# Top-2 dispatch on one core: row groups of 67 and 61 without an early store, in place of 65 and 63 with one

## The chip, the cores and the metric

The kernel runs on one core of one Trainium2 chip. The metric is the device time of one execution in microseconds. All transfers between the chip's main memory (HBM) and the on-chip memory (SBUF, 128 partitions) go through the core's 16 DMA engines; VectorE (DVE) and ScalarE (ACT) compute; SyncE (SP) and ACT issue transfers.

## What is computed

For each of 16 x 1024 tokens there are 8 router logits and a row of 512 float32 values. The two largest softmax probabilities are normalised to a sum of 1, and the row is written twice, scaled by each of the two weights, the smaller one first.

```python
probs = np.exp(router_logits - logits_max)
probs = probs / np.sum(probs, axis=-1, keepdims=True)
topk_indices = np.argsort(probs, axis=-1)[..., -k:]          # k = 2
topk_probs = np.take_along_axis(probs, topk_indices, axis=-1)
topk_probs = topk_probs / np.sum(topk_probs, axis=-1, keepdims=True)
x_expanded = x[:, :, np.newaxis, :].repeat(k, axis=2)
return (x_expanded * topk_probs[..., np.newaxis]).astype(np.float32)
```

So 33.6 MB of rows are read and 67.1 MB are written: each row that comes in goes out twice.

## The kernel before, in words

**Tiling.** 16384 tokens are 128 rows for each of the 128 partitions. They are handled in two groups, `GROUPS` (L16): 65 rows per partition, then 63. Within a group each partition owns consecutive tokens, so what one DMA moves for a partition is one contiguous piece. "A row" below means one row in each of the 128 partitions: 262,144 bytes of input and twice that of output.

**Homes.** `xs` (L97) holds one group's rows, one slot of 2 KB a row and partition; group 1 reuses the slots of group 0. `osp` (L98) has `OSP` output rows of 4 KB. Before the first output needs them, its last row holds the logits and the two rows before that the scratch space of the weights (L101, L102). A store's product lies either in `osp`, or in `xs` itself ("x"): the output pairs are written over input slots already used, and two slots hold one output row.

**Order.** For each group the loop at L109 first lists the loads of `LOADS[g]` (L112), one DMA each on SP's queue. In group 0 the logits come right behind the first load (L105, L106), and `top2_weights` (L53 to L68) finds the two largest logits by a small tournament on DVE; two sigmoids on ACT of their difference give the weights `WA`. Then come the stores of `STORES[g]`. Each has a count of rows, a home, `by_act` and a queue: one DVE multiplication (L127) does all rows but the last `by_act`, which ACT does in two copies a row (L135). Then the DMA at L138 goes out on the queue named.

In the texts, loads are numbered 1 to 5 and the stores on SP's queue by their order. Before, group 0 has loads 1 to 3 (6, 28, 31 rows), an early store of 2 rows, the only DMA issued by ACT, and stores 1 to 4 (16, 16, 16, 15 rows); group 1 has loads 4 and 5 (32, 31 rows) and stores 5 to 8 (16, 16, 16, 15).

**What orders the work.** The framework puts in the waits from the slots that instructions share. A multiplication waits for the load of its rows. Stores alternate between `osp` and `xs`, so the multiplication for an `osp` store waits until the previous `osp` store has landed. A load of group 1 waits until the stores from the slots it overwrites have landed. SP takes its instructions in order: what waits at its head holds up all behind it.

Of the kernel before, what the change touches and what calls it, by code (L numbers as in the profile page):

```python
# [1 line left out]

# [4 lines left out]

F32 = mybir.dt.float32
ALU = mybir.AluOpType
ACTF = mybir.ActivationFunctionType  # L10
P = 128
E = 8
D = 512


GROUPS = [65, 63]  # L16
M = sum(GROUPS)


LOADS = [[6, 28, 31], [32, 31]]  # L20


STORES = [
    [
        (2, ("osp", 0), 0, "ACT"),
        (16, ("osp", 2), 0, "SP"),
        (16, ("x", 2), 0, "SP"),
        (16, ("osp", 0), 4, "SP"),
        (15, ("x", 35), 0, "SP"),
    ],  # L30
    [
        (16, ("osp", 0), 1, "SP"),
        (16, ("x", 0), 0, "SP"),
        (16, ("osp", 0), 4, "SP"),
        (15, ("x", 33), 0, "SP"),
    ],
]
OSP = 18


def top2_weights(nc, scratch, logits, WA):

    used = [0]

    def cut(n):
        a = scratch[:, used[0] : used[0] + M * n].rearrange("p (m n) -> p m n", n=n)
        used[0] += M * n
        return a

    a, b = logits[:, :, 0:4], logits[:, :, 4:8]  # L50
    hi = cut(4)
    lo = b
    nc.vector.tensor_tensor(hi, a, b, op=ALU.max)  # L53
    nc.vector.tensor_tensor(lo, a, b, op=ALU.min)  # L54
    n = 4
    while n > 1:
        n //= 2
        a, b = hi[:, :, 0:n], hi[:, :, n : 2 * n]
        nhi, nlo, tmp = cut(n), cut(n), cut(n)
        nc.vector.tensor_tensor(tmp, lo[:, :, 0:n], lo[:, :, n : 2 * n], op=ALU.max)  # L60
        nc.vector.tensor_tensor(nlo, a, b, op=ALU.min)  # L61
        nc.vector.tensor_tensor(nlo, nlo, tmp, op=ALU.max)  # L62
        nc.vector.tensor_tensor(nhi, a, b, op=ALU.max)  # L63
        hi, lo = nhi, nlo
    dlt = cut(1)
    nc.vector.tensor_tensor(dlt, hi, lo, op=ALU.subtract)  # L66
    nc.scalar.activation(WA[:, :, 0], dlt[:, :, 0], ACTF.Sigmoid, scale=-1.0)  # L67
    nc.scalar.activation(WA[:, :, 1], dlt[:, :, 0], ACTF.Sigmoid, scale=1.0)  # L68


@with_exitstack
def kernel(
    ctx: ExitStack,
    tc: tile.TileContext,
    x: bass.AP,
    router_logits: bass.AP,
    k: bass.AP,
    out: bass.AP,
):
    nc = tc.nc  # L80
    N = x.shape[0] * x.shape[1]
    assert int(k) == 2 and router_logits.shape[-1] == E and x.shape[2] == D
    assert N == P * M
    xf = x.rearrange("b s d -> (b s) d")
    of = out.rearrange("b s k d -> (b s) k d")
    rf = router_logits.rearrange("b s e -> (b s) e")
    x_v, o_v, rl_v = [], [], []
    t0 = 0
    for n in GROUPS:
        t1 = t0 + P * n  # L90
        x_v.append(xf[t0:t1].rearrange("(p m) d -> p m d", p=P))
        o_v.append(of[t0:t1].rearrange("(p m) k d -> p m k d", p=P))
        rl_v.append(rf[t0:t1].rearrange("(p m) e -> p m e", p=P))
        t0 = t1

    pool = ctx.enter_context(tc.tile_pool(name="pool", bufs=1))
    xs = pool.tile([P, max(GROUPS), D], F32)  # L97
    osp = pool.tile([P, OSP, 2, D], F32)  # L98
    WA = pool.tile([P, M, 2], F32)

    logits = osp[:, OSP - 1].rearrange("p k d -> p (k d)").rearrange("p (m e) -> p m e", e=E)  # L101
    scratch = osp[:, OSP - 3 : OSP - 1].rearrange("p r k d -> p (r k d)")  # L102

    def load_logits():
        nc.sync.dma_start(logits[:, : GROUPS[0]], rl_v[0])  # L105
        nc.sync.dma_start(logits[:, GROUPS[0] :], rl_v[1])  # L106

    m0 = 0
    for g, G in enumerate(GROUPS):  # L109
        r = 0  # L110
        for n in LOADS[g]:
            nc.sync.dma_start(xs[:, r : r + n, :], x_v[g][:, r : r + n, :])  # L112
            if g == 0 and r < 6 <= r + n:
                load_logits()
                top2_weights(nc, scratch, logits, WA)
            r += n
        assert r == G
        r = 0
        for n, (home, a), by_act, queue in STORES[g]:
            if home == "x":  # L120
                og = xs[:, a : a + 2 * n, :].rearrange("p (r k) d -> p r k d", k=2)
            else:
                og = osp[:, a : a + n]
            v = n - by_act
            w = WA[:, m0 + r : m0 + r + n, :]
            if v:
                nc.vector.tensor_tensor(  # L127
                    og[:, :v],
                    xs[:, r : r + v, :].unsqueeze(2).to_broadcast([P, v, 2, D]),
                    w[:, :v].unsqueeze(3).to_broadcast([P, v, 2, D]),  # L130
                    op=ALU.mult,
                )
            for i in range(v, n):
                for c in range(2):
                    nc.scalar.activation(  # L135
                        og[:, i, c], xs[:, r + i, :], ACTF.Copy, scale=w[:, i, c : c + 1]
                    )
            {"SP": nc.sync, "ACT": nc.scalar}[queue].dma_start(o_v[g][:, r : r + n], og)  # L138
            r += n
        assert r == G  # L140
        m0 += G


# [1 line left out]
_INS = ['x', 'router_logits', 'k']  # L145
_OUTS = [((16, 1024, 2, 512), 'float32')]

_NUMBERS = {'k': 2}


# [26 lines left out]
```

## Time and profile before

| | us |
|---|---|
| median of 3 runs | 239.23 (239.12 to 239.34) |
| the profiled execution: its own time | 239.38 |
| its span, first to last instruction | 237.6 |
| DVE busy in it | 132.2 (56%) |
| ACT busy in it | 13.2 (6%) |

The mean rate of the DMA engines over the span is 426 GB/s, reads and writes together. "q1" is the queue on which SP issues, "q10" that of ACT. In the timeline a row gives start, duration, engine (a "q" behind it: the issue of a DMA), line, operation, output and input, and in brackets how long the engine was idle before and what ended that. In the grouped lines the numbers behind the bar are the busy time, the mean of one in ns, and the idle time before. In the DMA issues the last number is the time from issue to landing. In the windows view, the last two columns are the share of the 16 DMA engines' time and the rate, of the packets that start in the stretch; a packet is what one partition moves in one DMA.

### The profile page before, as it was taken

The numbers are of one execution on the slowest core, as the hardware profiler recorded it, in microseconds if no ns is written. First come the engines' busy times: TensorE is split into PE (matmuls) and PEld (weight loads), VectorE is DVE, ScalarE is ACT, GpSimd is POOL, SyncE is SP. The second block draws the span as 40 slices with busy tenths as digits, with TensorE's granted clock in tenths as the row PEclk, the third lists the DMA queues.
The fourth block names the chain that finished last, engine by engine and source line by source line (L and its number), as shares of the span: only waits on it lengthen the run. The fifth ranks groups of instructions, "written<-read, shape, count | busy, mean of one in ns | idle before, by whom it ended". The sixth has DMA issues, their size and how long they took to land.

```text
span 237.6 us, 124 instructions
## 1 busy us (share of the span) xinstructions
DVE 132.2 (56%) x20; ACT 13.2 (6%) x21; POOL 0.2 (0%) x4
## 2 busy tenths in 40 slices
DVE  0640599999289999000000009999956999920000
ACT  2000000000080000000000001000006100000000
POOL 0000000000000000000000000000000000000000
DMA  7979989898989989899998989898989989897995
GB/s 265 541 338 488 408 386 535 348 530 353 496 386 441 441 353 530 353 508 414 414 519 353 508 370 502 353 519 353 496 386 419 463 353 530 353 530 342 496 445 217
DMA packets 2304, 101.19 MB, mean 426 GB/s; under 512 B 256, under 2 KB 384, under 8 KB 512
## 3 DMA queue, kind: packets, MB, share of 16 engines
q1 hardware_dynamic: 2160, 100.14, 97.7%
q10 hardware_dynamic: 144, 1.05, 1.0%
HBM read 34.08 MB, written 67.11 MB: 426 GB/s over the span
## 4 chain that ended last, share of the span: by engine, by line
DMA 48%; DVE 39%; SPq 1%; issue 0%; DVEq 0%
DMA xs<-in_x_dram 30%; DVE osp L127 25%; DMA out_dram<-osp 19%; DVE xs L127 14%; SPq L105 0%; SPq L106 0%; SPq L112 0%; SPq L138 0%; DVEq L127 0%
## 5 line engine op out<-in xcount | busy, mean ns | idle before, releaser
L127 DVE TENSOR_TENSOR osp<-xs,WA 128x12288 f32<-128x12288 f32 (+3 forms) x5 | 61.6, 12318 | 68.7 <-DMA xs<-in_x_dram 58.4
L127 DVE TENSOR_TENSOR xs<-xs,WA 128x16384 f32<-128x16384 f32 (+1 forms) x4 | 66.8, 16692 | 0.3
L135 ACT ACTIVATE osp<-xs,WA 128x512 f32<-128x512 f32 x18 | 11.4, 709 | 161.3 <-DMA out_dram<-osp 90.0
L53 DVE TENSOR_TENSOR osp<-osp 128x512 f32<-128x512 f32 x1 | 0.7, 692 | 8.2 <-DMA osp<-in_router_logits_dram 8.2
L67 ACT ACT_TABLE_LOAD x1 | 1.3, 1283 | 0.7 <-PEq L158 0.7
L67 ACT ACTIVATE WA<-osp 128x128 f32<-128x128 f32 x1 | 0.3, 316 | 10.1 <-DVE osp L66 10.1
L54 DVE TENSOR_TENSOR osp<-osp 128x512 f32<-128x512 f32 x1 | 0.7, 693 | 0.0
L60 DVE TENSOR_TENSOR osp<-osp 128x256 f32<-128x256 f32 (+1 forms) x2 | 0.7, 352 | 0.0
L62 DVE TENSOR_TENSOR osp<-osp 128x256 f32<-128x256 f32 (+1 forms) x2 | 0.7, 352 | 0.0
L63 DVE TENSOR_TENSOR osp<-osp 128x256 f32<-128x256 f32 (+1 forms) x2 | 0.7, 352 | 0.0
L61 DVE TENSOR_TENSOR osp<-osp 128x256 f32<-128x256 f32 (+1 forms) x2 | 0.7, 351 | 0.0
L66 DVE TENSOR_TENSOR osp<-osp 128x128 f32<-128x128 f32 x1 | 0.3, 292 | 0.0
L68 ACT ACTIVATE WA<-osp 128x128 f32<-128x128 f32 x1 | 0.3, 298 | 0.0
L158 POOL MEMSET const-bfloat16-1.0<- 128x1 bf16 x1 | 0.1, 102 | 0.0
L158 POOL MEMSET const-uint8-127<- 128x1 uint8 x1 | 0.1, 102 | 0.0
L158 POOL MEMSET const-float32-0.0<- 128x1 f32 x1 | 0.1, 99 | 0.2 <-issue 0.2
L158 POOL MEMSET const-float32-1.0<- 128x1 f32 x1 | 0.1, 99 | 0.0
## 6 DMA issues: line engine op xcount, KB each, us to landing
xs<-in_x_dram SPq DMA_DIRECT2D x2, 7936.0 KB, 40.8
out_dram<-xs SPq DMA_DIRECT2D x2, 7680.0 KB, 27.5
xs<-in_x_dram SPq DMA_DIRECT2D x1, 7168.0 KB, 24.2
xs<-in_x_dram SPq DMA_DIRECT2D x1, 1536.0 KB, 6.0
out_dram<-osp ACTq DMA_DIRECT2D x1, 1024.0 KB, 24.5
osp<-in_router_logits_dram SPq DMA_DIRECT2D x1, 260.0 KB, 6.2
osp<-in_router_logits_dram SPq DMA_DIRECT2D x1, 252.0 KB, 6.4
out_dram<-osp SPq DMA_DIRECT2D x4, 23.9
```

Of the source, the lines that this page charges most:

```text
L53: nc.vector.tensor_tensor(hi, a, b, op=ALU.max)
L54: nc.vector.tensor_tensor(lo, a, b, op=ALU.min)
L60: nc.vector.tensor_tensor(tmp, lo[:, :, 0:n], lo[:, :, n : 2 * n], op=ALU.max)
L61: nc.vector.tensor_tensor(nlo, a, b, op=ALU.min)
L62: nc.vector.tensor_tensor(nlo, nlo, tmp, op=ALU.max)
L63: nc.vector.tensor_tensor(nhi, a, b, op=ALU.max)
L66: nc.vector.tensor_tensor(dlt, hi, lo, op=ALU.subtract)
L67: nc.scalar.activation(WA[:, :, 0], dlt[:, :, 0], ACTF.Sigmoid, scale=-1.0)
L68: nc.scalar.activation(WA[:, :, 1], dlt[:, :, 0], ACTF.Sigmoid, scale=1.0)
L127: nc.vector.tensor_tensor(og[:, :v], xs[:, r : r + v, :].unsqueeze(2).to_broadcast([P, v, 2, D]), w[:, :v].unsqueeze(3).to_broadcast([P, v ...
L135: nc.scalar.activation(og[:, i, c], xs[:, r + i, :], ACTF.Copy, scale=w[:, i, c : c + 1])
L158: nc = _bacc.Bacc("TRN2", target_bir_lowering=False, num_devices=1)
```

## The change

The groups become 67 and 61 rows. The early store on ACT's queue is taken out, all DMAs are issued by SP, and the rows are cut anew: group 0 has loads 1 to 3 of 6, 31 and 30 rows and stores 1 to 5 of 14, 13, 13, 13 and 14; group 1 has loads 4 and 5 of 31 and 30 rows and stores 6 to 9 of 15, 15, 16 and 15. `osp` has 16 rows in place of 18, `xs` 67 slots in place of 65. The tables name each load's slot and each store's first row and slot; as given, the slots are the same as the rows.

```diff
-GROUPS = [65, 63]
+GROUPS = [67, 61]
 M = sum(GROUPS)
-LOADS = [[6, 28, 31], [32, 31]]
+LOADS = [[(6, 0), (31, 6), (30, 37)], [(31, 0), (30, 31)]]
 STORES = [
     [
-        (2, ("osp", 0), 0, "ACT"),
-        (16, ("osp", 2), 0, "SP"),
-        (16, ("x", 2), 0, "SP"),
-        (16, ("osp", 0), 4, "SP"),
-        (15, ("x", 35), 0, "SP"),
+        (0, 14, 0, ("osp", 0), 0, "SP"),
+        (14, 13, 14, ("x", 0), 0, "SP"),
+        (27, 13, 27, ("osp", 0), 3, "SP"),
+        (40, 13, 40, ("x", 27), 0, "SP"),
+        (53, 14, 53, ("osp", 0), 4, "SP"),
     ],
     [
-        (16, ("osp", 0), 1, "SP"),
-        (16, ("x", 0), 0, "SP"),
-        (16, ("osp", 0), 4, "SP"),
-        (15, ("x", 33), 0, "SP"),
+        (0, 15, 0, ("osp", 0), 1, "SP"),
+        (15, 15, 15, ("x", 0), 0, "SP"),
+        (30, 16, 30, ("osp", 0), 4, "SP"),
+        (46, 15, 46, ("x", 31), 0, "SP"),
     ],
 ]
-OSP = 18
+OSP = 16
...
-        for n in LOADS[g]:
-            nc.sync.dma_start(xs[:, r : r + n, :], x_v[g][:, r : r + n, :])
+        for n, s in LOADS[g]:
+            nc.sync.dma_start(xs[:, s : s + n, :], x_v[g][:, r : r + n, :])
...
-        r = 0
-        for n, (home, a), by_act, queue in STORES[g]:
+        for r, n, s, (home, a), by_act, queue in STORES[g]:
...
-                    xs[:, r : r + v, :].unsqueeze(2).to_broadcast([P, v, 2, D]),
+                    xs[:, s : s + v, :].unsqueeze(2).to_broadcast([P, v, 2, D]),
...
-                        og[:, i, c], xs[:, r + i, :], ACTF.Copy, scale=w[:, i, c : c + 1]
+                        og[:, i, c], xs[:, s + i, :], ACTF.Copy, scale=w[:, i, c : c + 1]
```

More of the change, by code (lines that the diff above doesn't have):

```diff
@@ L135 @@
                     nc.scalar.activation(
-                        og[:, i, c], xs[:, r + i, :], ACTF.Copy, scale=w[:, i, c : c + 1]
+                        og[:, i, c], xs[:, s + i, :], ACTF.Copy, scale=w[:, i, c : c + 1]
                     )
             {"SP": nc.sync, "ACT": nc.scalar}[queue].dma_start(o_v[g][:, r : r + n], og)
-            r += n
-        assert r == G
         m0 += G
```

## The prediction

> **What bounds the kernel now.** I read the page first: the DMA queues, then the chain.
>
> ```profile
> span 237.6 us, 124 instructions
> ...
> DMA packets 2304, 101.19 MB, mean 426 GB/s; under 512 B 256, under 2 KB 384, under 8 KB 512
> ## 3 DMA queue, kind: packets, MB, share of 16 engines
> q1 hardware_dynamic: 2160, 100.14, 97.7%
> q10 hardware_dynamic: 144, 1.05, 1.0%
> ...
> DMA 48%; DVE 39%; SPq 1%; issue 0%; DVEq 0%
> ```
>
> The chain gives VectorE (DVE) 39%, which suggests that compute bounds a third of the time. The queues speak against it: the two together keep all 16 DMA engines busy for 98.7% of the span. The chain passes through DVE because it follows waits; where DVE is on it, the DMA engines are working off something queued earlier. To see whether a hole hides in the average, I asked the windows view for stretches cut at the places where packets begin. It counts a packet where it starts, so a short window can read 0.00 or far over 1 without meaning idle time or overload.
>
> ```profile
> core 0: us, DVE busy (x) ACT busy (x) POOL busy (x), PEclk, DMA share, GB/s
> 0.00:1.70 1.70, 0.00 (x0) 0.97 (x1) 0.20 (x4) 1.00 0.00 0
> 7.18:45.73 38.55, 25.46 (x14) 0.51 (x2) 0.00 (x0) 1.00 1.01 431
> 45.73:217.86 172.13, 106.72 (x7) 11.36 (x18) 0.00 (x0) 1.00 1.00 434
> ```
>
> From 45.73 on the share is 1.00 at 434 GB/s for 172 us: no hole in which a better order could win anything. At that rate 101.19 MB takes 233.2 us; with 1.7 us before the first packet that is 234.9 of the 237.6 us. All that any order of the same bytes can win lies in the remaining 2.7 us: the slow beginning, the 431 GB/s of the stretch from 7.18 to 45.73, and the end.
>
> **The change part by part.** The bytes stay: 128 rows in, 256 rows out, the logits. So do 5 loads of x, 2 of logits, 9 stores, and with them the packets (144 each). What could move is how evenly they follow each other.
>
> *The early store goes.* It is the only transfer of the second queue. Its issue (size, us to landing), then the first large multiplication, the issue of store 1 behind it, and that store's time to landing:
>
> ```profile
> out_dram<-osp ACTq DMA_DIRECT2D x1, 1024.0 KB, 24.5
> ```
>
> ```profile
> 26.35 17.23 DVE L127 TENSOR_TENSOR osp<-xs,WA 128x16384 f32<-128x16384 f32 x1 [11.43 <-DMA xs<-in_x_dram]
> 43.61 0.35 SPq L138 DMA_DIRECT2D out_dram<-osp  x1
> ```
>
> ```profile
> out_dram<-osp SPq DMA_DIRECT2D x1, 22.2
> ```
>
> Its 1 MB needs 24.5 us to land, mixed packet by packet with loads 2 and 3. One row of x is 262,144 bytes, 0.604 us at 434 GB/s; one output row is 1.208. Loads 2 and 3 (28 and 31 rows) and the early store (2 output rows, worth 4) are 63 rows, 38.05 us. The trace has 38.55 from the first packet of load 2 to the first of store 1: 0.50 us over. By the rates, 3 of 434 GB/s over 38.55 us is 0.27 us. This stretch is the only one with two queues and the only long one before the last store under 434. I read the excess as the price of switching between the queues and expect it to go: a gain of 0.27 to 0.50 us; I take **0.35**, nearer to the lower, since the first engine's packets exaggerate and the window also catches the last small packets of the logits. From below the bound is zero: if it belongs to the beginning, it stays. The DVE work and the ACT issue that it saves lay beside the loads and are worth nothing.
>
> A rule weighed against this: the Trainium skill, "DMA: Bandwidth & Descriptors", section "Issuing engines are not separate DMA queues", says that transfers issued by several engines run on the same 16 DMA engines and interleave, and that this saves only issue time; then dropping the second queue moves nothing, and the sum would be 0 in place of 0.35. The trace agrees on the interleaving (24.5 us to land); whether it is free is rival 1.
>
> *Store 1 starts when loads 2 and 3 are done: is it ready?* This was the early store's other service: it filled 2.4 us in which DVE worked. Durations of DVE:
>
> ```profile
> L127 DVE TENSOR_TENSOR xs<-xs,WA 128x16384 f32<-128x16384 f32 x2 | 34.5, 17225 | 0.1
> L127 DVE TENSOR_TENSOR xs<-xs,WA 128x15360 f32<-128x15360 f32 x2 | 32.3, 16158 | 0.2
> L127 DVE TENSOR_TENSOR osp<-xs,WA 128x12288 f32<-128x12288 f32 x2 | 25.9, 12958 | 9.8 <-DMA out_dram<-osp 9.8
> ```
>
> 16, 15 and 12 rows are 17.23, 16.16 and 12.96 us: 1.067 us a row and 0.15 once. So 14 rows take 15.1, 13 rows 14.0, 10 rows 10.8. Load 2 with 31 rows runs from 7.18 for 18.7 us: the first engine is through at 25.9. Engines are up to 0.5 us apart:
>
> ```profile
> 43.82:45.73 1.91, 1.91 (x1) 0.00 (x0) 0.00 (x0) 1.00 0.00 0
> 45.73:46.20 0.47, 0.47 (x1) 0.00 (x0) 0.00 (x0) 1.00 5.16 2231
> 157.97:159.90 1.93, 1.84 (x2) 0.00 (x0) 0.00 (x0) 1.00 0.00 0
> 159.90:160.35 0.45, 0.45 (x1) 0.00 (x0) 0.00 (x0) 1.00 5.40 2330
> ```
>
> so the last one ends near 26.4, and with an estimated 0.4 us to landing and 0.1 to DVE (store 1 before: 45.73 plus 16 rows is 65.06, the last engine 65.5, landed 43.61 plus 22.2, or 65.8), store 1's multiplication runs from 26.9 to 42.0. Load 3 (30 rows, 18.1 us) frees the first engine at 44.0. Slack from issue to need: 2.0 us. How much is enough? Before, store 1 was issued at 43.61 and began at 45.73, 2.1 us, without a hole; store 5 is the tighter case:
>
> ```profile
> 142.10 16.16 DVE L127 TENSOR_TENSOR osp<-xs,WA 128x15360 f32<-128x15360 f32 x1 [46.93 <-DMA xs<-in_x_dram]
> ...
> 158.32 0.34 SPq L138 DMA_DIRECT2D out_dram<-osp  x1
> ```
>
> issued at 158.32, first packet at 159.90: 1.6 us, share still 1.00. In an empty queue (first load, below) it is 1.0. So 2.0 suffices; the cover is 0.4 to 1.0 us.
>
> *Smaller stores on two homes.* Store 3 (13 rows into `osp`) and store 5 (14 rows) wait until the store two before has landed, as before:
>
> ```profile
> 65.95 12.96 DVE L127 TENSOR_TENSOR osp<-xs,WA 128x12288 f32<-128x12288 f32 x1 [5.11 <-DMA out_dram<-osp]
> 78.98 0.33 SPq L138 DMA_DIRECT2D out_dram<-osp  x1
> 79.01 16.16 DVE L127 TENSOR_TENSOR xs<-xs,WA 128x15360 f32<-128x15360 f32 x1
> ```
>
> Store 1 lasts 16.9 us to 60.9; landing by 61.8; DVE does 10 rows by 72.7 beside ACT's 3; store 2 (15.7 us) ends at 76.6: slack 3.9. Store 4 in place, 14.0 more: 86.7 against 92.3. Store 5: from 93.2, 10 rows by 104.1, against 108.0: 3.9. Nothing starves, so the sum here is 0. ACT's 24 copies in place of 18 stand beside DVE and are shorter:
>
> ```profile
> L135 ACT ACTIVATE osp<-xs,WA 128x512 f32<-128x512 f32 x18 | 11.4, 709 | 161.3 <-DMA out_dram<-osp 90.0 <-DMA xs<-in_x_dram 71.2
> ```
>
> 8 copies in at most 5.7 us beside 10.8.
>
> *Load 4 waits for a later store.* Its slots 0 to 30 now overlap stores 2 and 4 (slots 0 to 25, 27 to 52), formerly one store. Behind it on SP stand load 5 and the stores of group 1.
>
> ```profile
> 95.20 0.33 SPq L138 DMA_DIRECT2D out_dram<-xs  x1
> 95.58 27.65 SPq L112 DMA_DIRECT2D xs<-in_x_dram  x2
> ```
>
> ```profile
> SPq L112 <- DMA out_dram<-xs: 26.2, 1, 26.2
> ```
>
> Before, load 4 went out right after store 4 and load 5 sat 26.2 us on SP for that store. Now both wait, till about 108.9. Store 5, issued at 104.1 ahead of them, keeps the engines busy from 108.0 to 124.9: 16 us of cover; cost 0. If store 5 stood behind load 4, the cover would be gone: rival 3.
>
> *Group 1.* Load 4 (31 rows) ends at 143.6, load 5 (30 rows) at 161.7. Store 6 may start after load 4's landing: 144.5 plus 0.1 and 15.1 for DVE's 14 rows, 159.7: slack 2.0, against 1.6 before. Stores 7 to 9 have 4 us and more, by the same arithmetic. The last store has 15 rows as before, so the tail is unchanged.
>
> Sum: -0.35 against the profiled execution's 239.38, which gives 239.03. That execution lies 0.15 us over the median; from 239.23 it is **238.9 us**. The starting order, the 1.7 us before the first packet and the 1.8 us outside the span stay.
>
> **Rivals.**
>
> *1. No gain (239.2).* The excess of 0.27 to 0.50 us comes with the first long load, not with the second queue. For it: the beginning is slow anyway. Against: the only other long load-after-load stretch (loads 4 and 5) lies in the window at 434. Within 0.2%.
>
> *2. Store 1 comes late (240.0, slower).* Place: the end of load 3. The early store no longer stretches the loads, so if DVE issues store 1 later than 44.0 less the needed 1.0 to 1.6 us, that is after 42.4 to 43.0, all 16 engines stand still, and every microsecond is one of the kernel: nothing later has slack to give it back. Load 2 landing 1.5 us later than worked out would put the issue at 43.5 and cost up to 1.1: 240.0 with the 0.35 still won. Against it: before, 1.6 us of slack left no hole.
>
> *3. Load 4 is queued ahead of store 5 (240.9, slower).* The source lists store 5 first; whether the built program keeps that order on SP is not to be seen here. If not, load 4 waits at SP's head for store 4's landing at 108.9, its first packet comes 1.0 to 1.6 us later, and the engines stand from 108.0 to 109.9 or 110.5: 1.9 to 2.5 us.
>
> ```profile
> 0.73 0.38 SPq L112 DMA_DIRECT2D xs<-in_x_dram  x1
> ```
>
> (1.0 is this issue at 0.73 against the first packets at 1.70.) Against it: before, SP kept store 4 ahead of load 4, though load 4's own store had landed 10 us earlier (issue 60.87 plus 24.3, below).
>
> ```profile
> 60.87 0.34 SPq L138 DMA_DIRECT2D out_dram<-xs  x1
> ```
>
> ```profile
> out_dram<-xs SPq DMA_DIRECT2D x1, 7680.0 KB, 27.7
> out_dram<-osp SPq DMA_DIRECT2D x2, 23.9
> out_dram<-xs SPq DMA_DIRECT2D x1, 24.3
> ```
>
> **How the numbers follow.** 0.2% of 239.23 is 0.48 us, about what a measurement of this kernel can tell from no change; the limits are 238.75 and 239.71. Forecast 0.64: with the gain between 0.27 and 0.50, a spread of runs of 0.1 either way, and engines that end up to 0.5 us apart, 0.28 of it falls under 238.75 and 0.36 above. Rival 1, 0.20: same. Rival 2, 0.10, and rival 3, 0.06: slower. Faster 0.28, same 0.56, slower 0.16. The range 238.5 to 239.7 holds forecast and rival 1 with both bounds of the gain and leaves out rivals 2 and 3.
>
> **What would show it.** No q10; between the first packet of load 2 and that of store 1 about 36.8 us at 434 GB/s; store 1 issued near 42.0 and its first packets near 44.0 without a hole; store 5 ahead of load 4 on SP; share 1.00 to the last store. A window without packets longer than one packet (some 2 us) near 44, 109 or 162 would make the prediction wrong, as would a rate under 434 in a stretch that has no hole.

## The result, and the profile after

The changed kernel is a little slower. Its median is 239.78 us (239.46 to 240.26), that of the kernel before on the same chip 239.30 (239.12 to 239.34): a ratio of 1.0023 [1.0014, 1.0032]. Measured once more it had 239.54 (239.35 to 240.14) beside 239.37, 1.0011 [1.0002, 1.0019]. The loss is thus 0.2 to 0.5 us, and its runs spread over 0.8 us where those of the kernel before spread over 0.2. The profiled execution took 239.65 us, with a span of 237.9, 0.3 longer than before.

The page of the changed kernel:

```profile
span 237.9 us, 131 instructions
...
DMA packets 2304, 101.19 MB, mean 425 GB/s; under 512 B 256, under 2 KB 384, under 8 KB 512
q1 hardware_dynamic: 2304, 101.19, 98.7%
```

Bytes and packets are as before, on one queue now, and it is as full as the two were together (98.7%). The page doesn't tell where 0.3 us went. The windows view of the changed kernel does, cut where the first packet of a transfer starts (columns as in the prediction): loads 2 and 3; stores 1 to 4; store 5; load 4; load 5; stores 6 to 8.

```profile
7.34:44.17 36.83, 20.89 (x13) 0.52 (x2) 0.00 (x0) 1.00 1.01 436
44.17:108.19 64.02, 47.73 (x4) 8.80 (x14) 0.00 (x0) 1.00 1.00 434
108.19:125.49 17.30, 0.00 (x0) 0.00 (x0) 0.00 (x0) 1.00 1.00 424
125.49:144.20 18.71, 0.00 (x0) 0.00 (x0) 0.00 (x0) 1.00 1.00 434
144.20:162.32 18.12, 17.07 (x2) 1.34 (x2) 0.00 (x0) 1.00 1.00 434
162.32:217.86 55.54, 43.30 (x3) 5.12 (x8) 0.00 (x0) 1.00 1.00 434
```

Below, a transfer's *stretch* is the time from its own first packet to the first packet of the next one, on the earliest engine, and what a stretch takes beyond its bytes at 0.604 us a row is its *excess*. Loads 2 and 3 are 61 rows, 36.84 us: the stretch has 36.83, and the excess of before is gone. Store 5 is 14 output rows, 16.91 us, and takes 17.30: 0.39 over, at 424 GB/s and a share of 1.00. The engines don't stand; some of its packets take longer. In the kernel before, the last store of group 0 (15 rows, 18.12 us) has next to no such excess (0.04):

```profile
103.68:121.84 18.16, 0.00 (x0) 0.00 (x0) 0.00 (x0) 1.00 1.00 433
```

The windows view also tells which packets are slow. Where a window holds one packet's start on each of the 16 engines, its share times its length is the mean time of these packets. Of store 5 of the changed kernel, the last packets but one and the last ones:

```profile
120.87:121.31 0.44, 0.00 (x0) 0.00 (x0) 0.00 (x0) 1.00 4.81 2085
122.98:123.42 0.44, 0.00 (x0) 0.00 (x0) 0.00 (x0) 1.00 5.69 2085
```

The former take 4.81 x 0.44, or 2.12 us, the latter 5.69 x 0.44, or 2.50. The whole excess of 0.39 lies in the last packet of each engine.

Added up: the first packet of load 2 starts 0.16 later (7.34 against 7.18), the loads give 0.50 (38.55 less 38.05), store 5 takes back 0.35 (0.39 less 0.04). So the earliest engine begins the last store at 217.86 in both kernels. What is left of the 0.3 us lies with the other engines. Windows at the start of the last store, first of the kernel before, then of the changed one:

```profile
217.86:218.30 0.44, 0.00 (x0) 0.00 (x0) 0.00 (x0) 1.00 5.17 2234
```

```profile
217.86:218.30 0.44, 0.00 (x0) 0.00 (x0) 0.00 (x0) 1.00 3.88 1676
218.30:219.00 0.70, 0.00 (x0) 0.00 (x0) 0.00 (x0) 1.00 0.81 351
```

A packet is counted where it starts, and here each has 61,440 bytes. 2234 GB/s over 0.44 us is 16 packets, so before, all 16 engines begin the last store within 0.44 us. After, 12 do, and 4 come later (351 GB/s over 0.70 us). The latest engine sets the end.

The order on SP is the one that was foreseen. Timeline of the changed kernel, SP's issues (those before store 1, stores 2 to 4 and 7 to 9 left out):

```profile
42.19 0.35 SPq L139 DMA_DIRECT2D out_dram<-osp  x1
...
104.27 0.33 SPq L139 DMA_DIRECT2D out_dram<-osp  x1
109.10 1.64 SPq L114 DMA_DIRECT2D xs<-in_x_dram  x2
160.32 0.34 SPq L139 DMA_DIRECT2D out_dram<-osp  x1
```

### The profile page after: what moved, and what is told of

Same layout as the page of the kernel before. It is cut to its first block, busy times and chain, and to the rows that moved or that the text cites. A ratio compares the mean times of both kernels' runs of the same rounds, so it can differ in the third digit from the quotient of the medians.

```text
span 237.9 us, 131 instructions
## 1 busy us (share of the span) xinstructions
DVE 129.0 (54%) x20; ACT 17.1 (7%) x27; POOL 0.2 (0%) x4
## 3 DMA queue, kind: packets, MB, share of 16 engines
q1 hardware_dynamic: 2304, 101.19, 98.7%
## 4 chain that ended last, share of the span: by engine, by line
DMA 52%; DVE 35%; SPq 1%; issue 0%; DVEq 0%
DMA xs<-in_x_dram 26%; DVE osp L128 23%; DMA out_dram<-osp 17%; DVE xs L128 13%; DMA out_dram<-xs 9%; SPq L107 0%; SPq L108 0%; SPq L114 0%; DVEq L128 0%; SPq L139 0%
## 5 line engine op out<-in xcount | busy, mean ns | idle before, releaser
L128 DVE TENSOR_TENSOR osp<-xs,WA 128x14336 f32<-128x14336 f32 (+2 forms) x5 | 64.8, 12959 | 73.2 <-DMA xs<-in_x_dram 55.8
L128 DVE TENSOR_TENSOR xs<-xs,WA 128x13312 f32<-128x13312 f32 (+1 forms) x4 | 60.4, 15092 | 0.3
L136 ACT ACTIVATE osp<-xs,WA 128x512 f32<-128x512 f32 x24 | 15.3, 711 | 157.4 <-DMA out_dram<-osp 92.4
```

The lines of the kernel that those rows point to most:

```text
L128: nc.vector.tensor_tensor(og[:, :v], xs[:, s : s + v, :].unsqueeze(2).to_broadcast([P, v, 2, D]), w[:, :v].unsqueeze(3).to_broadcast([P, v ...
L136: nc.scalar.activation(og[:, i, c], xs[:, s + i, :], ACTF.Copy, scale=w[:, i, c : c + 1])
```

## The experiments

The question is what slows the last packets of store 5, and what the early store had to do with it. Ratios stand against the kernel before, timed on the same chip. Where letters stand in the expectations: A1 is the pile-up of two loads issued at once, A2 the pitch of the slots, B the time at which load 4 is queued, C the size of the last store, D a price that is paid once, at the first place where stores and loads meet, E one that each such place costs, F that a transfer queued before the last packets of the one ahead have started slows them.

### Is the gain that of the second queue, and is the loss that of the pile-up or the pitch?

**The changed kernel again.** No edit.

> The changed kernel as it is, for a second profile and more times. Theory A (a lasting cost where store 5's last packets meet the queued loads of group 1, 0.39 us a DMA engine in the first profile of it): the stretch from the first packets of store 5 to the last of load 4 is again about 0.4 us longer than its bytes at 434 GB/s, and the time lies 0.3 to 0.6 us over the kernel before (239.6 to 239.9). Rival (the excess was an accident of one execution, and the loss lies at the start or the end): that stretch is within 0.05 us of its bytes, and another one is long.

239.54 us, as told above. Store 5 has its excess again (17.29 against 16.91), and 15 of the 16 engines begin the last store in time:

```profile
108.17:125.46 17.29, 0.00 (x0) 0.00 (x0) 0.00 (x0) 1.00 0.99 425
217.86:218.30 0.44, 0.00 (x0) 0.00 (x0) 0.00 (x0) 1.00 4.85 2095
```

So the excess on the earliest engine came again, and the lag of the other engines differs between these two executions.

**The early store on SP's queue**, in the kernel before:

```diff
-        (2, ("osp", 0), 0, "ACT"),
+        (2, ("osp", 0), 0, "SP"),
```

> The kernel before with one edit: its early store of 2 rows goes out on SP's queue, behind load 3, in place of ACT's. Theory of the prediction (the second queue costs 0.35 to 0.37 us between the first packet of load 2 and the first of store 1): this gap is gone, and the time is 238.9 to 239.0. Rival (the excess belongs to the first long load or to the early store itself): 239.2 to 239.35, with the stretch still 0.3 to 0.5 us over its bytes.

240.19 us, 1.0036 [1.0023, 1.0049]: one queue, and slower. SP issues the early store at 15.19 us, behind load 3, so it no longer mixes with the loads. Loads 2 and 3 alone (59 rows, 35.64 us) take 36.61: an excess of 1.0 us with a single queue. The second row is the last store of group 0, 18.12 by its bytes:

```profile
7.20:43.81 36.61, 24.55 (x14) 0.51 (x2) 0.00 (x0) 1.00 1.01 426
104.22:122.33 18.11, 0.00 (x0) 0.00 (x0) 0.00 (x0) 1.00 1.00 434
```

The excess lies in load 3's last packets, behind which the early store stands. In the kernel before, it lies mostly in load 2's last packets, beside which the early store runs; load 3, which alternates with it, does not pay. The first row is load 3's last packets here; the other two are of the kernel before, load 2's last packets and then load 3 with the early store:

```profile
40.48:41.21 0.73, 0.73 (x1) 0.00 (x0) 0.00 (x0) 1.00 4.63 1392
```

```profile
22.68:23.15 0.47, 0.00 (x0) 0.00 (x0) 0.00 (x0) 1.00 5.28 2004
25.79:36.40 10.61, 10.05 (x1) 0.00 (x0) 0.00 (x0) 1.00 1.06 458
```

Here a packet takes 4.63 x 0.73, or 3.38 us, where its 63,488 bytes are 2.34. In the kernel before, the packets that start in 22.68:23.15 take 5.28 x 0.47, or 2.48 us an engine, for bytes that are 2004 x 0.47 / 434, or 2.17: 0.31 of the 0.50 us. In 25.79:36.40, where two queues alternate, the rate divided by the share is 432 GB/s, full speed. So the price of "switching between the queues", on which the predicted gain rested, is refuted: without a switch the excess is larger, and where the queues alternate, load 3 runs at full speed. The rule that the prediction weighed (the Trainium skill, "DMA: Bandwidth & Descriptors", section "Issuing engines are not separate DMA queues": one set of engines, whoever issues, so that a second issuer saves only issue time) is borne out in part. The engines are shared, but this store's move to SP's queue cost 0.8 us (240.19 against 239.37): ACT's issue had bought it a place among the loads.

**Load 5 issued late**, in the changed kernel, so that loads 4 and 5 don't reach the queue together (a copy on ACT has to wait until store 5 has landed):

```diff
         for n, s in LOADS[g]:
+            if g == 1 and s == 31:
+                nc.scalar.activation(osp[:, 13, 0, 0:1], xs[:, 60, 0:1], ACTF.Copy)
```

> The changed kernel with load 5 held back until store 5 has landed (a one-element ACT copy from a slot of load 5 into an output slot of store 5 orders them), as load 5 was issued late before the change; load 4 is issued as in the changed kernel. Theory A1 (two loads piled up behind a store slow the store's last packets): the 0.4 us at the end of store 5 go away, 239.3 to 239.45. Theory A2 (the changeover costs this with load 4 alone, through the addresses or the homes): no difference from the changed kernel, 239.7 to 239.9. If load 5 comes too late there would be a hole near 144 us in the trace; it has 17 us.

239.80 us, 1.0015 [1.0007, 1.0024]. The excess stays, 17.26 against 16.91: it isn't the pile-up.

```profile
108.21:125.47 17.26, 0.00 (x0) 0.00 (x0) 0.00 (x0) 1.00 1.00 425
```

**The pitch of before**, `GROUPS = [65, 63]` with the changed kernel's scheme:

```diff
-LOADS = [[(6, 0), (31, 6), (30, 37)], [(31, 0), (30, 31)]]
+LOADS = [[(6, 0), (31, 6), (28, 37)], [(32, 0), (31, 32)]]
-        (53, 14, 53, ("osp", 0), 4, "SP"),
+        (53, 12, 53, ("osp", 0), 3, "SP"),
...
+        (0, 16, 0, ("osp", 0), 2, "SP"),
+        (16, 15, 16, ("x", 0), 0, "SP"),
+        (31, 16, 31, ("osp", 0), 4, "SP"),
+        (47, 16, 47, ("x", 31), 0, "SP"),
```

> Group sizes back to 65 and 63, everything else as in the changed kernel: no early store, loads 6, 31, 28 and 32, 31, stores 14, 13, 13, 13, 12 and 16, 15, 16, 16, osp of 16 rows, loads 4 and 5 issued together after store 4 has landed. Theory A2 (the distance between the partitions' pieces in HBM, which the group sizes set, makes the changeover slow): 238.9 to 239.3. Theory A1 (the pile-up of loads behind the store): no gain from it, 239.6 to 239.9, with the excess at the end of store 5.

241.11 us, 1.0076 [1.0063, 1.0090]. The last store of group 0 (12 rows, 14.50 us) has the largest excess yet, 0.64:

```profile
107.18:122.32 15.14, 0.00 (x0) 0.00 (x0) 0.00 (x0) 1.00 1.01 416
122.32:122.85 0.53, 0.00 (x0) 0.00 (x0) 0.00 (x0) 1.00 3.85 1608
```

The second row counts the engines that begin load 4 in time, in packets of 65,536 bytes: 13 of 16. So the pitch of before brings neither the excess nor the late engines to an end; it isn't the cause. What makes up the rest of this kernel's loss stays open.

### When load 4 is queued, and how large the store ahead of it is

**Load 4 late in the kernel before:** a copy on ACT holds it back until store 3 has landed, from 95.58 to 104.60 us.

```diff
         for n in LOADS[g]:
+            if g == 1 and r == 0:
+                nc.scalar.activation(osp[:, 11, 0, 0:1], xs[:, 0, 0:1], ACTF.Copy)
```

> The kernel before with load 4 held back until store 3 has landed (a one-element ACT copy from a slot of load 4 into a row of store 3), so that it is issued about 1 us after store 4's first packets, as load 4 stands to store 5 after the change; before, it was issued 8 us ahead of them. Theory B (the time of issue decides: a load issued into a running store slows that store's last packets): an excess of 0.25 to 0.8 us a DMA engine in the stretch of store 4, and 239.6 to 240.1. Theory C (the size of the last store decides: 15 rows cost nothing, 14 cost 0.25 to 0.4, 12 cost 0.8): excess under 0.1 us, 239.2 to 239.45.

239.24 us beside 239.16, 1.0004 [0.9995, 1.0013]: no difference. The store keeps to its bytes but for 0.1 us (18.22 against 18.12).

```profile
103.55:121.77 18.22, 0.00 (x0) 0.20 (x1) 0.00 (x0) 1.00 1.00 432
```

**Load 4 early in the changed kernel**: other cuts, so that no late store lies under its slots.

```diff
+LOADS = [[(6, 0), (31, 6), (30, 37)], [(30, 0), (31, 30)]]
...
+        (0, 16, 0, ("osp", 0), 2, "SP"),
+        (16, 15, 16, ("x", 0), 0, "SP"),
+        (31, 12, 31, ("osp", 0), 3, "SP"),
+        (43, 12, 43, ("x", 31), 0, "SP"),
+        (55, 12, 55, ("osp", 0), 3, "SP"),
```

> The groups of the changed kernel, cut so that load 4 (30 rows) shares slots with store 2 alone and is issued right behind store 5, some 3 us ahead of that store's first packets: stores 16, 15, 12, 12, 12 and 15, 15, 16, 15, loads 4 and 5 of 30 and 31 rows. The last store of group 0 has 12 rows. Theory B (time of issue): no excess at the end of store 5, 238.9 to 239.2. Theory C (size of the store): 0.8 us there, 239.8 to 240.2.

240.55 us, 1.0058 [1.0044, 1.0072], and 14.84 for 14.50: the excess (0.34) is there with an early load 4 as well.

```profile
110.57:125.41 14.84, 0.00 (x0) 0.00 (x0) 0.00 (x0) 1.00 1.01 424
```

**A last store of 15 rows**, in the changed kernel:

```diff
-        (40, 13, 40, ("x", 27), 0, "SP"),
-        (53, 14, 53, ("osp", 0), 4, "SP"),
+        (40, 12, 40, ("x", 27), 0, "SP"),
+        (52, 15, 52, ("osp", 0), 5, "SP"),
```

> The changed kernel with one row moved from store 4 to store 5: 14, 13, 13, 12, 15. Load 4 is issued late as in the changed kernel. Theory C (size of the last store): the excess falls from 0.25 to 0.4 us to under 0.1, 239.1 to 239.4. Theory B (time of issue): the excess stays, 239.5 to 239.8.

239.91 us, 1.0031 [1.0020, 1.0043]; 18.63 for 18.12. The size isn't it.

```profile
106.85:125.48 18.63, 0.00 (x0) 0.00 (x0) 0.00 (x0) 1.00 1.00 422
```

Neither size, nor pitch, nor the time of the load in the queue parts the kernels with the excess from those without. Up to here one thing does: the early store, on either queue.

### The early store alone

**Taken out of the kernel before:**

```diff
-        (2, ("osp", 0), 0, "ACT"),
-        (16, ("osp", 2), 0, "SP"),
+        (18, ("osp", 0), 0, "SP"),
```

> The kernel before with its early store taken out and nothing else put right: its two rows go to store 1, which then has 18 (two packets a partition in place of one). By the prediction's arithmetic load 3 ends at 43.1 and store 1 is multiplied until 44.6 and begins at 45.7 to 46.2: a hole of 2.6 to 3.2 us, less 0.35 for the early store's own cost: 241.4 to 242.1. If the early store had served no purpose: 238.9 to 239.3.

242.42 us, 1.0138 [1.0125, 1.0152]. Store 1 is issued at 44.41, too late, and load 3 (31 rows, 18.72 us) with the hole behind it takes 21.28: 2.5 us of standing engines. That is what the early store covered. And the last store of group 0, otherwise untouched, now has an excess: 18.68 where it had 18.16.

```profile
24.03:45.31 21.28, 20.25 (x2) 0.00 (x0) 0.00 (x0) 1.00 0.88 382
105.96:124.64 18.68, 0.00 (x0) 0.00 (x0) 0.00 (x0) 1.00 1.01 421
```

**Put back into the changed kernel**, on ACT's queue, the rest recut:

```diff
-        (0, 14, 0, ("osp", 0), 0, "SP"),
...
+        (0, 2, 0, ("osp", 0), 0, "ACT"),
+        (2, 14, 2, ("osp", 2), 0, "SP"),
+        (16, 13, 16, ("x", 0), 0, "SP"),
+        (29, 13, 29, ("osp", 0), 3, "SP"),
+        (42, 12, 42, ("x", 27), 0, "SP"),
+        (54, 13, 54, ("osp", 0), 4, "SP"),
```

> The changed kernel with the early store put back on ACT's queue (2 rows; then stores 14, 13, 13, 12, 13 in group 0), all else as changed: groups, loads, late issue of load 4, store 5 from osp. Theory D (the cost at the changeover from stores to loads is paid once, at the first place where stores and loads meet; the early store pays it during load 2, without it store 5 pays it): 0.3 to 0.4 us more in loads 2 and 3 than their bytes, under 0.1 at store 5; 239.2 to 239.4. Theory E (each place costs by itself; the changed cut of group 0 makes store 5's place dear): 0.3 to 0.4 at both; 239.9 to 240.2.

239.88 us, 1.0027 [1.0017, 1.0036]. The last store (13 rows, 15.70 us) takes 15.71 and is free of its excess, and loads 2 and 3 with the early store (65 rows' worth, 39.26 us) have one again, 0.76:

```profile
7.30:47.32 40.02, 25.01 (x14) 0.51 (x2) 0.00 (x0) 1.00 1.01 428
110.14:125.85 15.71, 0.00 (x0) 0.00 (x0) 0.00 (x0) 1.00 1.00 434
```

Taken out it appears, put back it goes: in these two edits an early store and a free passage from the last store to load 4 go together (one exception follows below). The home of the last store isn't it: it is `xs` in the first kernel, which pays, and `osp` in the second, which doesn't. And what the early store saves there, it takes at the loads. Of the kernel with the early store put back, load 2's last packets and load 3's:

```profile
24.48:25.10 0.62, 0.00 (x0) 0.00 (x0) 0.00 (x0) 1.00 4.44 1744
44.65:45.03 0.38, 0.38 (x1) 0.00 (x0) 0.00 (x0) 1.00 7.20 2587
```

Worked out as above, the former take 0.26 us longer than their bytes, beside the early store, the latter 0.47, with store 1 queued behind them since 43.51: 0.73 of the 0.76. That price at the loads and price at the last store are of one size is how a gain of 0.50 us came to nothing.

### What slows a transfer's last packets?

**A second passage from store to load**: ten rows of load 5 are queued behind store 6.

```diff
-LOADS = [[(6, 0), (31, 6), (30, 37)], [(31, 0), (30, 31)]]
+LOADS = [[(6, 0), (31, 6), (30, 37)], [(31, 0), (20, 31)]]
-        (0, 15, 0, ("osp", 0), 1, "SP"),
+        (0, 15, 0, ("osp", 0), 7, "SP"),
...
+            if g == 1 and r == 0:
+                nc.sync.dma_start(xs[:, 51:61, :], x_v[1][:, 51:61, :])
```

> The changed kernel with a second changeover from a store to a load: load 5 is cut in two, and its last 10 rows are loaded behind store 6 (whose multiplication is done in time by giving 7 of its rows to ACT). Theory D (paid once): 0.25 to 0.45 us at the end of store 5, under 0.1 at the end of store 6; 239.5 to 239.9. Theory E (each changeover costs): 0.25 to 0.45 us at both; 239.8 to 240.3.

241.90 us, 1.0113 [1.0098, 1.0128]. Store 5 has its excess of 0.5 (17.42); store 6 (15 rows, 18.12 us), also followed by a load, has none (18.14); the 10-row load, behind which store 7 has long been queued, takes 6.66 for 6.04.

```profile
108.06:125.48 17.42, 0.00 (x0) 0.00 (x0) 0.00 (x0) 1.00 0.99 421
156.28:174.42 18.14, 14.21 (x1) 1.33 (x2) 0.00 (x0) 1.00 1.00 434
174.42:181.08 6.66, 4.67 (x1) 3.79 (x6) 0.00 (x0) 1.00 1.00 381
```

**A small load among the stores** (the logits once more, behind store 2), to see whether the price can be paid ahead:

```diff
+    again = pool.tile([P, max(GROUPS), E], F32)
...
+            if g == 0 and r == 14:
+                nc.sync.dma_start(again, rl_v[0])
```

> The changed kernel with one more small load, group 0's logits once more into a tile of its own (0.27 MB, 0.65 us), queued between stores 2 and 3. Theory D (paid once, at the first load behind a store): the excess moves to the end of store 2, and store 5 ends with under 0.1; 240.2 to 240.6. Theory E: store 5 still 0.25 to 0.45 us over its bytes, whatever the small load costs; 240.2 to 241.0.

240.22 us, 1.0042 [1.0030, 1.0055]. Store 5 still has 0.27 over, 17.18. So a small load doesn't pay ahead; whether a large one would was not tried.

**Load 4 queued late, on either side of the last packets' start.** Fillers on DVE, eight of two rows and one of one row, or seven of two rows, hold load 4 back (the first is shown):

```diff
         for n, s in LOADS[g]:
+            for v in 8 * [2] + [1] if g == 1 and s == 0 else []:
+                nc.vector.tensor_tensor(
+                    osp[:, 14 : 14 + v],
+                    osp[:, 0:v],
+                    xs[:, 0:v].unsqueeze(2).to_broadcast([P, v, 2, D]),
+                    op=ALU.mult,
+                )
```

An engine moves 8 of a transfer's 128 packets of rows, so a packet of store 5 takes 16.91 / 8, 2.1 us, and the last ones start some 2.1 to 2.5 us before its stretch ends at 125.5: at 123.0 to 123.4.

> The changed kernel with load 4 held back until about 123.9 us: nine filler multiplications on DVE behind store 5's (into two free rows, 19.5 us in all), of which load 4 waits for the last. At that time store 5's last packets (from 123.0 on) are already running. Theory F (a transfer of the other direction that stands in the queue when the last packet starts slows that packet; queued later it does not): the 0.25 to 0.4 us at the end of store 5 are gone, the first packets of load 4 come at 125.2 to 125.6 without a hole, 239.1 to 239.4. Theory G (it is the first large changeover from stores to loads that costs, whenever the load is queued): still 0.25 to 0.45 us there, 239.5 to 239.9. If issue to first packet needs more than 1.4 us, a hole adds the rest.

240.08 us, 1.0035 [1.0021, 1.0048]. Issued at 124.09, after that start, load 4 leaves store 5 alone (16.95), but its own stretch now has 19.49 for 18.72.

```profile
108.12:125.07 16.95, 15.71 (x8) 0.00 (x0) 0.00 (x0) 1.00 1.00 433
125.07:144.56 19.49, 0.00 (x0) 0.00 (x0) 0.00 (x0) 1.00 1.00 417
```

> The same with seven fillers: load 4 is issued at about 120.4 us, 2.6 us before store 5's last packets start and 11 us later than in the changed kernel. Theory F: the excess of 0.25 to 0.4 us stays, since load 4 is queued in time to be seen; 239.5 to 239.9. If the excess is gone here too, it hangs on how long the load has been waiting and not on the last packet: 239.1 to 239.4. Theory G: stays.

239.97 us, 1.0035 [1.0023, 1.0048]. Issued at 120.36, before that start, it leaves the excess with store 5:

```profile
108.08:125.49 17.41, 12.08 (x6) 0.00 (x0) 0.00 (x0) 1.00 1.00 422
```

The pair shows which packets pay at this passage from a store to a load: the last ones of the store if the load is queued before they start; else the first ones of the load, and those pay more (0.77 against 0.27 to 0.51 for this store in the runs here). That the time would fall to 239.1 to 239.4 didn't come true.

**Store 1 a little later, with the early store.** In the kernel with the early store put back, a multiplication of one row ahead of store 1's delays its issue from 43.51 to 44.53:

```diff
+            if g == 0 and r == 2:
+                nc.vector.tensor_tensor(
+                    osp[:, 2:3],
+                    xs[:, 36:37].unsqueeze(2).to_broadcast([P, 1, 2, D]),
+                    WA[:, 0:1].unsqueeze(3).to_broadcast([P, 1, 2, D]),
+                    op=ALU.mult,
+                )
```

> The changed kernel with the early store back on ACT's queue, and store 1 delayed by one more multiplication of a row (1.2 us), so that it is issued at about 45.0 in place of 43.8, when load 3's last packets (from 44.7 on) have mostly started. Theory F: the 0.47 us at the end of load 3 that the early store's return brought are gone or at most 0.15, and the time falls from 239.88 to 239.3 to 239.6. Theory G or any cause that does not hang on when store 1 is queued: 0.4 to 0.5 us there as before, 239.8 to 240.0.

The loads' excess falls from 0.76 to 0.27 (39.53 for 39.26), which the reading demands. The time doesn't follow: 240.52 us, 1.0056 [1.0043, 1.0069]. The last store of group 0 (15.70 by its bytes) has 0.17 over, although the early store runs among the loads: an exception to what the two edits above showed. And in the profiled execution (241.09 us) one engine falls far behind. One begins load 4 after 126.00, where the earliest does at 125.44. One, probably the same, begins a packet of the last store but one (65,536 bytes, 2.42 us) as late as 217.6, so its part of the last store begins at about 220.0; the earliest begins that at 217.8.

```profile
7.22:46.75 39.53, 24.64 (x15) 0.51 (x2) 0.00 (x0) 1.00 1.01 433
109.57:125.44 15.87, 0.00 (x0) 0.00 (x0) 0.00 (x0) 1.00 1.01 429
126.00:127.00 1.00, 0.00 (x0) 0.00 (x0) 0.00 (x0) 1.00 0.16 63
217.60:217.70 0.10, 0.00 (x0) 0.00 (x0) 0.00 (x0) 1.00 1.51 655
```

**The first store of group 1 earlier, in the kernel before.** Load 5 has 31 rows there, a packet takes 18.72 / 8, 2.34 us, and the last ones start at 157.56 (159.90 less 2.34) to 157.96. Store 5 is issued at 158.32, just behind them. One more row by ACT brings it to 157.35, ahead of them:

```diff
-        (16, ("osp", 0), 1, "SP"),
+        (16, ("osp", 0), 2, "SP"),
```

> The kernel before with one number changed: in store 5, the first of group 1, ACT does 2 rows in place of 1, so DVE does 14 and the store is issued 1.07 us earlier, at about 157.25. Theory F (a store issued more than about 0.2 us before a load's last packet starts slows that packet): load 5's last packets start at 157.6 to 158.0 on all 16 engines, so all are slowed by 0.2 to 0.7 us, and the kernel gets slower by being early: 239.5 to 239.9. Rival H (more slack does no harm, as the prediction assumed): no excess there, 239.15 to 239.35.

239.98 us, 1.0021 [1.0012, 1.0030]: a store that is ready 1 us *sooner* costs as much as the whole change. The time is near what theory F gave, but it had all 16 engines slowed, and that didn't come true. Below are the issue, the two of load 5's last packets that start latest, 0.5 us and more after the issue, and the first packets of the store, here of 65,536 bytes.

```profile
157.35 0.34 SPq L138 DMA_DIRECT2D out_dram<-osp  x1
```

```profile
157.84:158.20 0.36, 0.36 (x1) 0.00 (x0) 0.00 (x0) 1.00 0.95 353
159.78:160.30 0.52, 0.52 (x1) 0.00 (x0) 0.00 (x0) 1.00 4.09 1765
```

The two packets take 0.95 x 0.36 x 16 / 2, or 2.74 us each, in place of 2.34. 14 of the 16 engines begin the store within 0.52 us, and two are late. In the kernel before itself, all 16 begin the store within the same 0.52 us, and its first packets take 4.67 x 0.52, or 2.43 us, for 2.42 by their bytes: a store that is queued behind the start of a load's last packets slows neither these nor its own.

```profile
159.90:160.42 0.52, 0.52 (x1) 0.00 (x0) 0.00 (x0) 1.00 4.67 2017
```

The changed kernel stands in between: its load 5 has packets of 2.27 us, the last ones start at 160.05 to 160.56, and store 6 is issued at 160.32, in the midst of them; 15 engines begin store 6 in time (1772 GB/s over 0.52 us), one doesn't. Of load 5's last packets, the one that starts latest takes 3.13 x 0.05 x 16, or 2.50 us, 0.23 over:

```profile
160.55:160.60 0.05, 0.05 (x1) 0.00 (x0) 0.00 (x0) 1.00 3.13 1229
162.32:162.84 0.52, 0.52 (x1) 0.00 (x0) 0.00 (x0) 1.00 4.10 1772
```

**Store 6 later in the changed kernel**, by a small filler on DVE, or by giving ACT's row to DVE:

```diff
+            if g == 1 and r == 0:
+                nc.vector.tensor_tensor(
+                    osp[:, 15, 0, 0:352], xs[:, 0, 0:352], xs[:, 1, 0:352], op=ALU.mult
+                )
```

> The changed kernel with a small DVE instruction (352 elements, about 0.5 us) ahead of store 6's multiplication, so that store 6 is issued at about 160.85 in place of 160.3, after the last packet of load 5 has started on every engine (160.05 to 160.6) and still 1.4 us before the first engine is free. Theory F: no engine's last packet is slowed, the latest engine ends 0.25 to 0.35 us after the mean in place of 0.3 to 0.5, and the time falls by 0.1 to 0.3 us: 239.4 to 239.6. Rival H: 239.5 to 239.8 as the changed kernel, or 0.5 more if the slack was needed.

```diff
-        (0, 15, 0, ("osp", 0), 1, "SP"),
+        (0, 15, 0, ("osp", 0), 0, "SP"),
```

> The changed kernel with all 15 rows of store 6 on DVE (none on ACT), which issues it 1.07 us later, at about 161.4, 0.95 us before the first engine is free. Theory F: no slowed last packet, but the wait from issue to first packet (1.0 to 1.6 us by the prediction, under 1.0 by the kernel with 65 and 63 rows, which had 0.86 and a hole of 0.09) may leave a hole of up to 0.2 us: 239.4 to 239.7. Rival H with 1.6 us needed: a hole of 0.65 us, 240.1 to 240.4.

239.72 us, 1.0020 [1.0011, 1.0029], and 239.68, 1.0015 [1.0006, 1.0024]: neither wins the time back. In the first, store 6 is issued at 161.45, later than planned; two engines are late already at load 4's first packets (63,488 bytes each; 14 and 2), and two still at the last store (61,440 bytes each, 14 begin within 0.44 us):

```profile
125.41:125.93 0.52, 0.00 (x0) 0.00 (x0) 0.00 (x0) 1.00 3.96 1709
217.86:218.30 0.44, 0.00 (x0) 0.00 (x0) 0.00 (x0) 1.00 4.53 1955
```

In the second the store came too late in the profiled execution: issued at 162.43, it left a hole of about 1.0 us behind load 5 (19.13 for 18.12).

```profile
144.13:163.26 19.13, 16.98 (x2) 0.00 (x0) 0.00 (x0) 1.00 0.95 411
```

No version that was tried beats the kernel before.

## Why the prediction was wrong

- **The gain at the loads**: there, and larger than taken (0.50 on the earliest engine, where 0.35 was booked). Its reason was wrong. The excess isn't the price of two queues, since it is 1.0 us with one. It lies in a load's last packets while a store stands or runs beside them: 0.31 of the 0.50 us in load 2's, beside the early store. In the kernel with the early store put back, that is 0.26, and store 1, queued before load 3's last packets start, adds 0.47.
- **"Store 1 starts when loads 2 and 3 are done: is it ready?"**: right. Issue at 42.19 (42.0 was said), first packets at 44.17 (44.0), no hole. Rival 2 didn't happen.
- **The order on SP**: right. Store 5 (104.27) stays ahead of load 4 (109.10); rival 3 didn't happen.
- **"Load 4 waits for a later store": cost 0.** This step failed. "16 us of cover" asked whether the engines would stand, and they don't. But a passage from stores to loads has a price without any hole: 0.39 us, in packets that take longer. The kernel before hides it (0.04), and the prediction took that for granted in any order. But the passage was free together with the early store, the very thing the change removes. The prediction named the sign, "a rate under 434 in a stretch that has no hole".
- **"Stores 7 to 9 have 4 us and more ... so the tail is unchanged"**: failed by about 0.27 us, the 239.65 less 239.38 of the profiled executions, of which the earliest engine lost 0.01. The stores had their slack; the engines weren't level. The packet that was slowed by 0.23 when store 6 was queued is on the engine that was latest then. Slack of 2.0 us for store 6 "against 1.6 before" was booked as harmless, and in the kernel before 1 us more of it costs 1.0021 [1.0012, 1.0030].
- The sum, against the profiled executions: -0.35 was said and +0.27 came. The difference of 0.62 is 0.16 at the start, -0.15 at the loads, 0.35 at store 5 and 0.27 in the latest engine, within rounding. The first of these looks like chance: load 2 begins at 7.20, 7.21, 7.22 and 7.30 in four of the other kernels here.

**What stays open.** Shown is that taking the early store out makes the passage from the last store to load 4 cost, and putting it back makes it nearly free; with store 1 delayed as well it cost 0.17 again. Why is not shown: pile-up, pitch, size, home and the time of issue are excluded, a small load among the stores doesn't do the same, and the second passage of one kernel was free without it. That the price is paid once (D) would fit most of this: where the loads' last packets had paid 0.31, 0.73 or 1.0 us, the later passage cost 0.04 at most; where the loads had an excess of 0.27, it cost 0.17; where they had none, 0.27 to 0.64. But no run tells it from other effects of the early store. The late engines of the changed kernel were not removed by any run alone: delaying store 6 didn't level them, and in that run two were late already at load 4's first packets.

## What to carry to other kernels

Where the DMA engines are full, look at the places where loads turn to stores and back: ask of each stretch whether it takes longer than its bytes though its share is 1.00, and of the last transfer how many engines begin it in time. A transfer that looks like a mere filler can also set what a passage 76 us later costs (from 45.73, where the loads end, to 121.84 here), so an edit that removes it is to be priced there, too. And more slack for a transfer isn't always safer: queued before the last packets of a transfer of the other direction have started, it can slow them.

## What the runs showed of the hardware

- A transfer of the other direction, queued before the last packets of the one ahead have started, made some of these take longer in most of the passages here: 0.27 to 0.64 us for the last store of group 0 in the kernels without the early store, 0.6 for a load of ten rows, and, by the same reading but not tried apart, 1.0 for load 3 with the early store behind it. Not in all: it was 0.04 and 0.10 for the last store of group 0 in the kernel before and in that kernel with load 4 late, and 0.02 for store 6 ahead of the ten-row load.
- Queued after that start, a load took the price on its own first packets (0.77 us); a store, the first of group 1 in the kernel before, took none (2.43 us a packet for 2.42).
- Engines that fell behind didn't catch up: in one kernel two of 16 were late at load 4's first packets and two at the last store, 92 us later, with every engine busy in between.
